# A hybrid decoder trunk on one core: the first Strassen step of each FFN takes two products of plain blocks first, and sums of weight blocks are made when first asked for

## The chip, the core and the metric

The kernel runs on one core of a Trainium2 chip. A time is that of one execution of the whole program on the device, in microseconds (us). The core's engines run side by side and wait for each other through semaphores: PE (matrix products), DVE and ACT (elementwise work), POOL (a little elementwise work) and SP (it issues nearly all DMAs). Each engine takes its instructions strictly in the order in which the program lists them.

## The reference

One step of a decoder trunk of two layers over 544 tokens (512 of a prompt, 32 of eight sampled sequences). Each layer has two half-weighted SwiGLU FFNs around a mixer, four FFNs in all, and ends in a gated embedding:

```python
def swiglu(x, w1, w3, w2):
    return (jax.nn.silu(x @ w1) * (x @ w3)) @ w2
...
h = h + 0.5 * swiglu(rmsnorm(h, ffn1_norm[i]), ffn1_w1[i], ffn1_w3[i], ffn1_w2[i])
```

The model width is 1024 and the FFN width 2816. The mixer of layer 0 is a chunked gMLP, that of layer 1 an attention with forget gates whose K and V come once from the end of layer 0.

## The kernel before, in words

**Values in two parts.** All of it is float32. An operand is split into a rounded part `hi` (a cast on ACT, L190 for weights) and the rest `lo` (a subtraction on DVE, L191), and a product is three passes: hi·hi, hi·lo, lo·hi. So each 128x1024 piece of weights costs a DMA, one cast and one subtraction before PE can use it.

**An FFN.** It starts with four plain products over all of K (`tile_mm`: L233, L237, L239, 48 matmuls each), which make the first 256 of the 2816 hidden columns. The other 2560 come in ten steps of 256 columns (`ffn_steps`, L476), each by the Strassen-Winograd scheme: seven products of 24 matmuls instead of eight. Each step handles W1 and W3 together. Products are named by the digits "1" to "7":

- "1", "2", "4" multiply plain weight blocks a11, a12, a22. "5" takes a21+a22, "6" takes ("5" - a11), "7" takes a11-a21, "3" takes a12 - "6" (`seven`). Each such sum is one DVE instruction of 1.22 us (L176, in `_sum`).
- They add up in three accumulators of PSUM: "1", "6", "7", "4" in A, "5", "3" in C (both of the pool `ps`, three buffers, which the four plain products use too), "2" in B (two buffers of the pool `pb`).
- What "1", "6" and "5" leave in A and C is copied out by ACT (L484, here r1, r6, r5) before the next product adds to the same accumulator. So "6" waits for r1 and "7" for r6.

**The order of weights.** `ffn_pieces` lists all pieces in the order in which PE takes them; `prepare` runs ahead in that list. Before unit u it splits pieces up to u+2, makes sums up to u+3, and issues the loads that piece u+6 needs:

```python
p = self.pieces[min(u + load, end)]
need = [x for x in (p["sum"][::2] if p["sum"] else [p["src"]]) if isinstance(x[1], int)]
```

A raw block that was not asked for in this way is loaded when its split or sum asks for it (`_raw`). Raw blocks are loaded in the order a11, a21, a22, a12.

**The order of work.** The four plain products are ordered by a scheduler, and the steps behind them stand as the code issues them. On DVE and ACT the start of an FFN is full: besides casts, subtractions and sums there are the input forms of the seven products (`forms`, L299 on ACT, L303 to L306 and L278 on DVE, L277 on ACT; four times) and the gates of the plain columns (L418 to L421), and L418 and L420 are what frees the `ps` buffers of the plain products. In the first FFN SP reads a page table into registers between DMAs (48 register loads, L914).

Of the kernel before, what the change touches and what calls it, by code (L numbers as in the profile page):

```python
# [26 lines left out]
ALU = mybir.AluOpType  # L27
# [25 lines left out]
NKP = NC_ // 2  # L53

SEVEN = "1562734"


ORDER = """
# [28 lines left out]
class Builder:  # L87
# [37 lines left out]
    def set_stream(self):  # L125
        self.chain, self.pending, self.bg, self.pages = None, [], [], {}
        self.aps, self.raws = [], {}
        self.pieces, self.sums, self.split = [], {}, {}
        self.p_next = self.p_split = self.p_sum = self.a_load = 0
        self.ahead = (2, 2, 4)  # L130
        self.pins = 0
# [9 lines left out]
    def seven(self, aps):  # L141

        r = len(self.aps)
        self.aps.extend(aps[k] for k in (0, 2, 3, 1))
        a11, a21, a22, a12 = ((r + k, 0) for k in range(4))
        d = {k: dict(key=(r, k), src=x, sum=None) for k, x in (("1", a11), ("2", a12), ("4", a22))}
        for k, x, op, y in (("5", a21, "+", a22), ("6", (r, "5"), "-", a11), ("7", a11, "-", a21),
                            ("3", a12, "-", (r, "6"))):
            d[k] = dict(key=(r, k), sum=(x, op, y))
        for v in d.values():  # L150
            v.update(n=1024)
        return d

    def _load(self):
# [12 lines left out]
    def _sum(self):  # L167
        p = self.pieces[self.p_sum]
        self.p_sum += 1
        if p["sum"] is None:  # L170
            return
        a, op, b = p["sum"]
        get = lambda x: self._raw(x, 1024) if isinstance(x[1], int) else self.sums[x]
        a, b = get(a), get(b)
        t = self.flat(1024)
        self.nc.vector.tensor_tensor(t, a, b, ALU.add if op == "+" else ALU.subtract)  # L176
        self.sums[p["key"]] = t

    def _split(self):
        while self.p_sum <= self.p_split:  # L180
# [181 lines left out]
    def ffn_slots(self):  # L362


        out, tail = [], len(PARTS) - 1
        for j in range(1, NPAIR):
            ws = [("w", p, c, None) for p, c in BETWEEN.get(j, ())]
            gs = [("g", j, k, None) for k in SEVEN]
            early = j % 2 == 1
            for n, g in enumerate(gs):  # L370
                out.append(g)
                if ws and n in ((0, 2, 4, 6) if early else (3, 4, 5, 6)):
                    out.append(ws.pop(0))
            assert not ws
        n = 2 * PARTS[tail]
        out += [("w", tail, c, range(n - 2)) for c in range(3)] + [("w", tail, c, range(n - 2, n)) for c in range(3)]
        return out + [("w", tail, c, None) for c in range(3, NC_)]
# [1007 lines left out]
```

## Time and profile before

| | |
|---|---|
| median of 3 runs | 2092.44 us (2092.16 to 2092.45) |
| the profiled execution | 2092.14 us, its span 2090.4 us (1.7 us lie outside the span) |
| mean granted TensorE clock | 0.997 of full speed |
| busy PE, DVE, ACT | 98%, 73%, 45% of the span |

The span runs from the first to the last instruction in the trace, and all positions below are us from its start. A row of the order of time names an engine's instruction and, in brackets, how long the engine had been idle before it and which instruction ended that.

### The profile page before, as it was taken

How to read it: one execution, taken by the hardware profiler on the slowest of the kernel's cores; microseconds unless marked ns; L12 is line 12 of the kernel's file. 1: busy time of each engine (PE TensorE's matmuls, PEld its weight loads, DVE VectorE, ACT ScalarE, POOL GpSimd, SP SyncE). 2: the span in 40 equal slices, each digit the busy share in tenths (PEclk: the TensorE clock that was granted, in tenths of full speed). 3: DMA queues.
4: the chain of work that ended last, by engine and by line, in shares of the span. 5: the costliest groups of instructions: out<-in, count | busy, mean ns of one | idle time of the engine just before them, and what ended most of it. 6: DMA issues, size and time to landing. Idle time of an engine off the chain costs nothing.

```text
span 2090.4 us, 38801 instructions
## 1 busy us (share of the span) xinstructions
PE 2056.4 (98%) x16364; PEld 2019.2 (97%) x16364; DVE 1521.3 (73%) x1893; ACT 935.0 (45%) x1376; POOL 179.0 (9%) x226
## 2 busy tenths in 40 slices
PE   7999999999999999999999999999999999999999
PEld 6999999999999999999999999999977999999999
DVE  7877787556787777776698777786465787777873
ACT  6444344423445344454355344444364654343451
POOL 0000000410100000042050000001041300000020
PEclk9999999999999999999999999999999999999999
DMA  4232324312223232432194332326467322322331
GB/s 162 91 112 71 111 92 141 104 54 71 72 101 117 73 105 81 152 97 81 48 327 143 111 101 91 112 78 198 158 197 264 102 102 71 111 83 99 123 102 44
DMA packets 93776, 237.94 MB, mean 114 GB/s; under 512 B 9490, under 2 KB 27442, under 8 KB 93602
## 3 DMA queue, kind: packets, MB, share of 16 engines
q1 hardware_dynamic: 93458, 235.42, 33.8%
q8 instruction: 129, 2.11, 0.4%
q14 instruction: 45, 0.37, 0.1%
q10 hardware_dynamic: 144, 0.04, 0.0%
HBM read 218.94 MB, written 16.49 MB: 113 GB/s over the span
## 4 chain that ended last, share of the span: by engine, by line
PE 89%; DVE 5%; ACT 3%; issue 1%; DMA 1%; POOL 1%; SPq 0%; ACTq 0%; DVEq 0%; POOLq 0%
PE ps L476 33%; PE ps L233 14%; PE ps L239 14%; PE ps L237 14%; PE pb L476 5%; ACT big L190 1%; DVE big L191 1%; DVE big L176 1%; PE ps L1144 1%; PE ps L1146 1%; PE ps L1145 1%; PE ps L992 0%; PE ps L990 0%; PE ps L1105 0%; ACT big L277 0%
## 5 line engine op out<-in xcount | busy, mean ns | idle before, releaser
L476 PE MATMUL ps<-big,big 128*128 128x272 f32 x5760 | 749.6, 289 | 9.7 <-ACT tmp L484 6.2
L476 PEld LDWEIGHTS ps<-big,big 128*128 128x128 f32 x5760 | 735.2, 189 | 11.5 <-ACT tmp L484 7.7
L191 DVE TENSOR_TENSOR big<-big,big 128x1024 fp32r<-128x1024 f32 (+2 forms) x541 | 594.1, 1100 | 101.2 <-ACT big L190 100.5
L190 ACT CAST big<-big 128x1024 fp32r<-128x1024 f32 (+2 forms) x541 | 489.2, 931 | 280.5 <-DVE big L176 275.7
L233 PE MATMUL ps<-big,big 128*128 128x256 f32 x2768 | 577.2, 290 | 13.9 <-ACT big L190 7.2
L237 PE MATMUL ps<-big,big 128*128 128x256 f32 x2768 | 571.8, 287 | 0.0
L239 PE MATMUL ps<-big,big 128*128 128x256 f32 x2768 | 571.6, 288 | 0.0
L233 PEld LDWEIGHTS ps<-big,big 128*128 128x128 f32 x2768 | 444.4, 189 | 17.3 <-ACT big L190 7.2
L237 PEld LDWEIGHTS ps<-big,big 128*128 128x128 f32 x2768 | 446.9, 189 | 0.0
L239 PEld LDWEIGHTS ps<-big,big 128*128 128x128 f32 x2768 | 443.5, 188 | 0.9 <-issue 0.4
L318 POOL TENSOR_TENSOR st<-st,tmp 128x544 f32<-128x544 f32 (+1 forms) x63 | 86.5, 1373 | 1611.6 <-ACT tmp L316 1611.3
L176 DVE TENSOR_TENSOR big<-big,big 128x1024 f32<-128x1024 f32 x160 | 194.9, 1218 | 0.0
L515 DVE SCALAR_TENSOR_TENSOR big<-ps,big 128x544 f32<-128x544 f32 x160 | 115.5, 722 | 106.8 <-PE ps L239 106.7
L484 ACT COPY tmp<-ps 128x544 f32<-128x544 f32 x120 | 73.5, 613 | 146.5 <-PE ps L476 146.2
L476 PE MATMUL pb<-big,big 128*128 128x272 f32 x960 | 127.1, 288 | 0.0
L448 ACT ACTIVATE big<-big 128x544 f32<-128x544 f32 x80 | 52.8, 661 | 161.8 <-DVE big L445 160.7
L476 PEld LDWEIGHTS pb<-big,big 128*128 128x128 f32 x960 | 123.2, 188 | 0.0
L289 ACT ACTIVATE big<-big,gains 128x544 fp32r<-128x544 f32 (+1 forms) x80 | 56.0, 704 | 124.3 <-DVE big L515 64.9
L445 DVE TENSOR_TENSOR big<-big,st 128x1088 f32<-128x1088 f32 x80 | 103.2, 1290 | 10.0 <-ACT big L498 8.5
L278 DVE TENSOR_TENSOR big<-big,big 128x544 fp32r<-128x544 f32 (+1 forms) x96 | 69.5, 724 | 28.8 <-ACT big L277 28.3
L290 DVE SCALAR_TENSOR_TENSOR big<-big,gains,big 128x544 fp32r<-128x544 f32 (+1 forms) x80 | 64.0, 804 | 27.7 <-ACT big L289 27.7
L277 ACT CAST big<-big 128x544 fp32r<-128x544 f32 (+1 forms) x96 | 61.9, 644 | 26.4 <-DVE big L769 14.9
(189 smaller groups left out, 1269.6 us busy)
## 6 DMA issues: line engine op xcount, KB each, us to landing
big<-in_w SPq DMA_DIRECT2D x160, 512.0 KB
big<-in_w2a SPq DMA_DIRECT2D x64, 512.0 KB
big<-in_w2b SPq DMA_DIRECT2D x32, 384.0 KB
big<-in_w13p SPq DMA_DIRECT2D x16, 512.0 KB
big<-in_win SPq DMA_DIRECT2D x16, 512.0 KB
big<-in_wg SPq DMA_DIRECT2D x16, 512.0 KB
big<-in_wkv SPq DMA_DIRECT2D x16, 512.0 KB
big<-in_ck SPq DMA_DIRECT2D x16, 512.0 KB
```

The lines of the kernel that those rows point to most:

```text
L176: self.nc.vector.tensor_tensor(t, a, b, ALU.add if op == "+" else ALU.subtract)
L190: self.nc.scalar.copy(hi, src)
L191: self.nc.vector.tensor_tensor(lo, src, hi.bitcast(F32), ALU.subtract)
L233: i = nc.tensor.matmul(out[:, a:b], wh, xh[:, a:b], start=s, stop=False)
L237: nc.tensor.matmul(out[:, a:b], wh, xl[:, a:b], start=False, stop=False)
L239: nc.tensor.matmul(out[:, a:b], wl, xh[:, a:b], start=False, stop=e)
L278: self.nc.vector.tensor_tensor(pair[:, 1, cols], src, pair[:, 0, cols].bitcast(F32), ALU.subtract)
L318: nc.gpsimd.tensor_tensor(acc[:, cols], acc[:, cols], sq, ALU.add)
L445: tt(g, g, rstd.unsqueeze(1).broadcast_to([P, 2, T]), ALU.mult)
L476: nc.tensor.matmul(dst[w], a[:, c], b, start=k in "152" and kp == 0 and n == 0, stop=kp == NKP - 1 and n == 2, skip_group_check=True)
L484: nc.scalar.copy(t["r" + k], t["C" if k == "5" else "A"])
L515: nc.vector.scalar_tensor_tensor(h[c], whole(out), 0.5, h[c], ALU.mult, ALU.add)
```

## The change

The ten steps of an FFN took the products in the order 1 5 6 2 7 3 4. The first step of each FFN now takes them as 1 2 6 5 7 3 4; the other nine stay. A sum that is needed before its own place in the list is made on the spot, with the sums it rests on, since "6" now stands ahead of "5". The count of instructions of every engine stays the same, and so do the bytes loaded.

```diff
--- before.py
+++ after.py
@@ -54,6 +54,8 @@
 
 SEVEN = "1562734"
 
+FIRST = "1265734"
+
 
 ORDER = """
 q0 K3 K2 K0 q1 q2 q3 K1 s0123 n2 n3 n1 q4 f1 p1 q5 q6 f0 n0 q7 p2 p0 f3 f2 a0 s4567 p3 t0 a1 v0 a2
@@ -125,7 +127,7 @@
     def set_stream(self):
         self.chain, self.pending, self.bg, self.pages = None, [], [], {}
         self.aps, self.raws = [], {}
-        self.pieces, self.sums, self.split = [], {}, {}
+        self.pieces, self.sums, self.defs, self.split = [], {}, {}, {}
         self.p_next = self.p_split = self.p_sum = self.a_load = 0
         self.ahead = (2, 2, 4)
         self.pins = 0
@@ -149,6 +151,7 @@
             d[k] = dict(key=(r, k), sum=(x, op, y))
         for v in d.values():
             v.update(n=1024)
+            self.defs[v["key"]] = v
         return d
 
     def _load(self):
@@ -167,14 +170,20 @@
     def _sum(self):
         p = self.pieces[self.p_sum]
         self.p_sum += 1
-        if p["sum"] is None:
-            return
-        a, op, b = p["sum"]
-        get = lambda x: self._raw(x, 1024) if isinstance(x[1], int) else self.sums[x]
-        a, b = get(a), get(b)
-        t = self.flat(1024)
-        self.nc.vector.tensor_tensor(t, a, b, ALU.add if op == "+" else ALU.subtract)
-        self.sums[p["key"]] = t
+        if p["sum"] is not None:
+            self._form(p)
+
+    def _form(self, p):
+
+        key = p["key"]
+        if key not in self.sums:
+            a, op, b = p["sum"]
+            get = lambda x: self._raw(x, 1024) if isinstance(x[1], int) else self._form(self.defs[x])
+            a, b = get(a), get(b)
+            t = self.flat(1024)
+            self.nc.vector.tensor_tensor(t, a, b, ALU.add if op == "+" else ALU.subtract)
+            self.sums[key] = t
+        return self.sums[key]
 
     def _split(self):
         while self.p_sum <= self.p_split:
@@ -365,7 +374,7 @@
         out, tail = [], len(PARTS) - 1
         for j in range(1, NPAIR):
             ws = [("w", p, c, None) for p, c in BETWEEN.get(j, ())]
-            gs = [("g", j, k, None) for k in SEVEN]
+            gs = [("g", j, k, None) for k in (FIRST if j == 1 else SEVEN)]
             early = j % 2 == 1
             for n, g in enumerate(gs):
                 out.append(g)
```

Where instructions stand now, at three places in the first FFN. The names carry the program's buffer numbers, which differ a little between the two programs, and the lines of the change are 9 higher.

**SP**, the loads of the first Strassen step's raw blocks; 175 is a11 (issued earlier), 258 is a21, 260 is a22, and a12 is 262 before and 409 in the change. Before:

```order
L157 DMA big_258<-in_w 128x1024
L157 DMA big_260<-in_w 128x1024
L157 DMA big_262<-in_w 128x1024
L914 TENSOR_LOAD pt
L914 ISA x2
...
L1241 DMA big_348<-in_passed 128x512
```

In the change:

```order
L160 DMA big_258<-in_w 128x1024
L160 DMA big_260<-in_w 128x1024
L923 TENSOR_LOAD pt
L923 ISA x2
...
L1250 DMA big_344<-in_passed 128x512
...
L160 DMA big_409<-in_w 128x1024
```

TENSOR_LOAD with its ISA row is one register load from the page table. Before, the three blocks are issued together, and 14 register loads follow up to in_passed. In the change a12 stands behind 15 register loads, in_passed and 5 more. The plain products are units 0 to 3 and "1" is piece 4. Before, unit 1 asks for piece 7, "2", and so for a12; in the change piece 7 is "5", which needs a21 and a22 alone, and a12 is asked for at unit 3, by the split of "2", now piece 5.

**DVE**, from the subtraction of "1" (the first row) to the forms of the last kp (the last row). Before, 414 is the subtraction of "5"; in the change 412 is that of "2". Before:

```order
L191 TENSOR_TENSOR big_341<-big_175,big_340 128x1024
L176 TENSOR_TENSOR big_344<-big_258,big_260 128x1024
L303 TENSOR_TENSOR tmp_402<-big_399 128x544
L305 TENSOR_TENSOR tmp_403<-big_399,tmp_402 128x272
L306 TENSOR_TENSOR tmp_403<-big_399,tmp_403 128x272
L278 TENSOR_TENSOR big_404<-tmp_402,big_404 128x544
L278 TENSOR_TENSOR big_405<-tmp_403,big_405 128x544
L191 TENSOR_TENSOR big_414<-big_344,big_413 128x1024
L176 TENSOR_TENSOR big_417<-big_344,big_175 128x1024
L303 TENSOR_TENSOR tmp_473<-big_470 128x544
```

In the change:

```order
L200 TENSOR_TENSOR big_339<-big_175,big_338 128x1024
L312 TENSOR_TENSOR tmp_398<-big_395 128x544
L314 TENSOR_TENSOR tmp_399<-big_395,tmp_398 128x272
L315 TENSOR_TENSOR tmp_399<-big_395,tmp_399 128x272
L287 TENSOR_TENSOR big_400<-tmp_398,big_400 128x544
L287 TENSOR_TENSOR big_401<-tmp_399,big_401 128x544
L200 TENSOR_TENSOR big_412<-big_409,big_411 128x1024
L184 TENSOR_TENSOR big_415<-big_258,big_260 128x1024
L184 TENSOR_TENSOR big_417<-big_415,big_175 128x1024
L312 TENSOR_TENSOR tmp_473<-big_470 128x544
```

The sum of "5" (344 before, 415 in the change) moved from ahead of the third forms to behind the subtraction of the step's second product, where it stands together with the sum of "6" (417 in both).

**ACT**, the casts and copies of the step, from the last cast of the gates on. Before, the casts are those of "6", "2", "7", "3" and "4" (520, 524, 559, 595, 627), and the copies are r1, r5 and r6 in this order:

```order
L277 CAST big_490<-tmp_485 128x544
L190 CAST big_520<-big_417 128x1024
L190 CAST big_524<-big_262 128x1024
L484 COPY tmp_557<-ps_495 128x544
L190 CAST big_559<-big_528 128x1024
L484 COPY tmp_593<-ps_532 128x544
L190 CAST big_595<-big_563 128x1024
L484 COPY tmp_625<-ps_495 128x544
L190 CAST big_627<-big_260 128x1024
```

In the change the casts are those of "6", "5", "7", "3" and "4" (520, 524, 560, 598, 629), and the copies are r1, r6 and r5:

```order
L286 CAST big_490<-tmp_485 128x544
L199 CAST big_520<-big_417 128x1024
L199 CAST big_524<-big_415 128x1024
L493 COPY tmp_558<-ps_495 128x544
L199 CAST big_560<-big_528 128x1024
L199 CAST big_598<-big_564 128x1024
L493 COPY tmp_627<-ps_495 128x544
L199 CAST big_629<-big_260 128x1024
L493 COPY tmp_659<-ps_602 128x544
```

The cast of "2" is gone from here, since it is earlier now, and that of "5" came. The copy r5 moved behind r6; r6 stands behind one cast more than r1 or two ("7", and now "3").

## Rows read from the trace of the kernel before

**Rows 1.** The page: busy time of each engine with its share of the span and its count of instructions, and the shares of the chain that ended last by engine.

```profile
PE 2056.4 (98%) x16364; PEld 2019.2 (97%) x16364; DVE 1521.3 (73%) x1893; ACT 935.0 (45%) x1376; POOL 179.0 (9%) x226
...
PE 89%; DVE 5%; ACT 3%; issue 1%; DMA 1%; POOL 1%; SPq 0%; ACTq 0%; DVEq 0%; POOLq 0%
```

**Rows 2.** The waits of PE over the whole span: engine and line, what it waited for, total us, times, longest.

```profile
PE ps L476 <- ACT tmp L484: 6.2, 7, 2.0
PE ps L233 <- DVE tmp L418: 4.2, 1, 4.2
PE ps L476 <- DVE tmp L418: 3.5, 1, 3.5
```

**Rows 3.** PE in order of time at the first Strassen step of the first FFN: start, us, engine, line, operation, out<-in, forms, how many, and in brackets the idle time before it and what ended that. These are the products "1", "5", "6", "2", and from 59.62 on "7" and what follows without a pause.

```profile
40.22 3.18 PE L476 MATMUL ps<-big,big 128*128 128x272 f32 x24
46.87 4.52 PE L476 MATMUL ps<-big,big 128*128 128x272 f32 x24 [3.47 <-DVE tmp L418]
52.11 3.28 PE L476 MATMUL ps<-big,big 128*128 128x272 f32 x24 [0.72 <-ACT tmp L484]
55.22 3.19 PE L476 MATMUL pb<-big,big 128*128 128x272 f32 x24
59.62 12.57 PE L476 MATMUL ps<-big,big 128*128 128x272 f32 x98 [1.20 <-ACT tmp L484]
```

**Rows 4.** DVE in order of time in the same stretch, columns as in rows 3.

```profile
36.92 1.23 DVE L191 TENSOR_TENSOR big<-big,big 128x1024 fp32r<-128x1024 f32 x1 [0.23 <-ACT big L190]
38.06 1.22 DVE L176 TENSOR_TENSOR big<-big,big 128x1024 f32<-128x1024 f32 x1
...
42.61 1.23 DVE L191 TENSOR_TENSOR big<-big,big 128x1024 fp32r<-128x1024 f32 x1
43.76 1.22 DVE L176 TENSOR_TENSOR big<-big,big 128x1024 f32<-128x1024 f32 x1
44.89 0.72 DVE L303 TENSOR_TENSOR tmp<-big 128x544 f32<-128x544 f32 x1
...
46.00 0.72 DVE L418 TENSOR_TENSOR tmp<-ps,st 128x544 f32<-128x544 f32 x1
...
50.64 2.36 DVE L191 TENSOR_TENSOR big<-big,big 128x1024 fp32r<-128x1024 f32 x2 [0.23 <-ACT big L190]
...
55.25 1.23 DVE L191 TENSOR_TENSOR big<-big,big 128x1024 fp32r<-128x1024 f32 x1 [1.11 <-ACT big L190]
56.39 1.22 DVE L176 TENSOR_TENSOR big<-big,big 128x1024 f32<-128x1024 f32 x1
```

**Rows 5.** ACT in order of time in the same stretch.

```profile
41.53 1.05 ACT L190 CAST big<-big 128x1024 fp32r<-128x1024 f32 x1
42.48 1.39 ACT L299 ACTIVATE big<-big,gains 128x544 f32<-128x544 f32 x2
...
49.56 1.99 ACT L190 CAST big<-big 128x1024 fp32r<-128x1024 f32 x2
51.45 0.60 ACT L484 COPY tmp<-ps 128x544 f32<-128x544 f32 x1
...
58.01 1.05 ACT L190 CAST big<-big 128x1024 fp32r<-128x1024 f32 x1 [2.28 <-DVE big L176]
58.96 0.60 ACT L484 COPY tmp<-ps 128x544 f32<-128x544 f32 x1
```

**Rows 6.** The DMAs that SP issues in the first 60 us, merged by line and tile; the second number is the time from the first issue to the end of the last one of the row, and SP's register loads are not shown by this view.

```profile
13.93 5.81 SPq L157 DMA_DIRECT2D big<-in_w13p  x2
19.78 9.35 SPq L157 DMA_DIRECT2D big<-in_w  x4
37.05 0.33 SPq L1241 DMA_DIRECT2D big<-in_passed  x1
```

**Rows 7.** POOL in order of time: the first reader of the tile that the DMA in_passed fills.

```profile
40.83 0.51 POOL L1244 CAST neg<-big 128x384 fp32r<-128x384 f32 x1 [27.47 <-DMA big<-in_passed]
```

**Rows 8.** Stretches of the span: from:to, length, busy time of PE, weight loads, DVE, ACT and POOL with their counts, granted TensorE clock (1.00 is 2.4 GHz, 0.50 is 1.2 GHz), share of the DMA engines, GB/s. The first two follow the issue at 13.93.

```profile
15.00:17.20 2.20, 2.20 (x19) 2.20 (x19) 1.99 (x4) 2.20 (x6) 0.00 (x0) 1.00 0.64 225
17.20:19.40 2.20, 2.20 (x20) 2.20 (x19) 1.89 (x4) 2.20 (x5) 0.00 (x0) 1.00 0.00 0
```

**Rows 9.** Stretches of the span, columns as in rows 8, behind three pauses of PE.

```profile
32.64:36.05 3.41, 3.41 (x15) 3.41 (x16) 2.88 (x6) 3.14 (x5) 0.00 (x0) 0.50 0.17 70
...
46.87:49.71 2.84, 2.84 (x12) 2.84 (x13) 2.75 (x6) 1.96 (x4) 0.00 (x0) 0.50 0.97 392
...
1688.10:1691.50 3.40, 3.40 (x17) 3.40 (x17) 2.29 (x3) 1.56 (x2) 0.00 (x0) 0.50 0.00 0
```

**Rows 10.** PE in order of time at the first Strassen step of the second FFN (products "1" and "5" in one row, "6", "7" and on) and, last, product "6" of the fourth FFN.

```profile
574.83 6.19 PE L476 MATMUL ps<-big,big 128*128 128x272 f32 x48
581.18 3.28 PE L476 MATMUL ps<-big,big 128*128 128x272 f32 x24 [0.16 <-ACT tmp L484]
...
588.33 3.90 PE L476 MATMUL ps<-big,big 128*128 128x272 f32 x29 [0.84 <-ACT tmp L484]
...
1687.20 4.80 PE L476 MATMUL ps<-big,big 128*128 128x272 f32 x24 [1.98 <-ACT tmp L484]
```

**Rows 11.** DVE in order of time in the second FFN, where the difference of a split waits for its cast.

```profile
571.69 1.23 DVE L191 TENSOR_TENSOR big<-big,big 128x1024 fp32r<-128x1024 f32 x1 [1.12 <-ACT big L190]
```

## The prediction

> **What bounds the kernel now.** I read the page first. PE is busy for 98% of the span and carries 89% of the chain that ended last [rows 1]; 2090.4 - 2056.4 leaves 34 us for all its pauses. Work that stays the same can therefore be made shorter only by taking pauses away, or the half clock behind them. The waits of PE come next [rows 2]: 6.2 us in seven waits of Strassen products for a copy out of PSUM (L484), 3.5 us in one wait of a Strassen product for L418, which frees a `ps` buffer, and 4.2 us in a wait of a plain product for L418 that lies ahead of the change's place. The second is the one that the new order touches most directly: "5" stands second now and must have a `ps` buffer, while "2" needs one of `pb`.
>
> The order of time shows where it lies [rows 3]: "5" starts at 46.87 after 3.47 us of pause and takes 4.52 us, where "1" took 3.18. Then "6" waits 0.72 for r1 and "7" 1.20 for r6, and behind 59.62 no pause follows. So everything that this stage does to the end is read at one point: when "7" starts.
>
> What sets "6" is the next question, since it stands third in both orders. DVE has hardly a gap from 36.92 to 50.64 [rows 4]; ACT has the cast of "6" at 49.56 and right behind it the copy r1, 51.45 + 0.60 = 52.05 [rows 5], and "6" starts at 52.11. The start of "6" thus goes by the chain of sums, forms, gates and casts on DVE and ACT, and not by how early PE is done with the product ahead of it.
>
> **Part 1: the load of a12 in the first FFN.** Before, a12 is the last of four loads whose issue ends at 29.13; a single issue takes 0.33, so it stands at 28.8 [rows 6]. The order of SP in the change puts 20 register loads and in_passed ahead of it. Fourteen register loads took 37.05 - 29.13 = 7.92 us [rows 6], so 0.566 each. The new issue stands at 28.8 + 20 x 0.566 + 0.33 = 40.45, 11.7 us later. Nothing waits in these register loads that a faster engine could shorten.
>
> From issue to use I have two prices. in_passed, of half the size, was issued at 37.05 and its first reader, POOL, started at 40.83 [rows 7]: 3.78. The two loads issued from 13.93 on moved their bytes by 17.2, behind which the DMA engines stand still [rows 8]: about 3.2. I take 3.5, since the queue is as empty at 40.45 as in these two cases, and keep 3.2 and 3.8 as ends. So a12 is there at 43.95. The Trainium skill (DMA: Bandwidth & Descriptors, Rules for kernel authors) advises to issue a DMA early, compute, and wait late; this edit does the reverse. By that rule the load is exposed, as the rows have it; were the load hidden all the same, the sum would be that of the second rival below.
>
> The cast of "2" stands on ACT where that of "5" stood, at 41.53 [rows 5], and now waits for 43.95. ACT and DVE work in order, so the forms and gates behind it wait too. The subtraction came 1.08 us behind its cast (41.53 to 42.61), and what follows it comes at a pace of 1.15 [rows 4]. So: subtraction 45.03; sum of "5" 46.18; sum of "6" 47.33, plus 0.2 because it now needs the result of the instruction right ahead of it (between nothing and 0.31, the overlap of 0.08 between neighbours plus the 0.23 that DVE waits at 36.92 for a result of ACT [rows 4]); the forms at 47.53 + 1.15 = 48.68, where they were at 44.89. That is 3.8 us, and the chain behind moves along: "6" starts at 52.11 + 3.8 = 55.9.
>
> PE in the meantime: "1" as before to 43.4, "2" from about 45.0, and even at half clock (24 x 0.227 = 5.45, from 15 matmuls in 3.41 us [rows 9]) it is done by 50.5. Then PE stands for more than 5 us, and "6" begins at half clock. What this costs, three places show: "5" 4.52 - 3.08 = 1.4 (98 matmuls take 12.57 us, so 24 take 3.08 [rows 3]); 15 x (0.227 - 0.128) = 1.5 behind the pause of 4.2 [rows 2, 9]; 4.80 - 3.2 = 1.6 in the fourth FFN [rows 10], with a granted clock of 0.50 in each [rows 9]. I take 1.6, as this pause is the longest; the upper end is a whole product at half clock, 5.45 - 3.08 = 2.4. Below, r6 sets the end: from the cast of "6" (49.56) to the end of r6 (59.56) lie 10.0 us [rows 5], so "7" can't start before 49.56 + 3.8 + 10.0 = 63.4.
>
> "6" and "5" then take 6.16 + 1.6 from 55.9, and "7" starts at 63.6 where it stood at 59.62: **+4.0 us** for the first FFN, between +3.25 and +5.2 with the ends above. The pause at "5" (3.47) and its half clock don't come back, as they lie ahead of the start of "6".
>
> **Part 2: the second FFN.** In the other three FFNs no register loads stand on SP, and a12 comes in time. In the second, "6" waits 0.16 and "7" 0.84 [rows 10]. DVE waits 1.12 us there for a cast at 571.69 [rows 11], between the subtraction of "5" and its sum; with "2" second, this subtraction still waits, but the sums and forms behind move up against the casts. I take the 0.16 and half of the 0.84: **-0.6 us**, between -1.0 and nothing.
>
> **Part 3: the third and fourth FFN.** The same counts of casts, sums and forms stand ahead of "6"; only the two sums of "5" and "6" now stand behind each other, 0.2 us each as above: **+0.4 us** in the two, between nothing and 0.6.
>
> **Part 4, at nothing.** The edit of `_sum` makes no other instruction. The copy r5, now behind r6, has all of "7" (3.1 us) to be done before "3" needs its accumulator; without that cover it would cost its 0.60. The cast of "3" ahead of r6 is inside the 10.0 us above.
>
> **Sum:** 4.0 - 0.6 + 0.4 = +3.8 on the profiled 2092.14 us, thus 2095.9. The three runs have a median 0.3 above the profiled execution, so 2096.2 in their terms. The ends: 3.25 - 1.0 = +2.3 and 5.2 + 0.6 = +5.8, so 2094.7 and 2098.2. About 0.2%, 4.2 us, is what a measurement of this kernel can tell from no change, and the forecast lies just inside it.
>
> **The rivals.** *The half clock lasts longer, and it is slower by over 0.2%.* Place: PE at "6" and "5" of the first FFN, behind more than 5 us of pause and a "2" that ran at half clock itself. For it speaks that no row of before has two such pauses so close; against it that all three pauses cost 1.4 to 1.6. It decides from a cost of 2.0 us on, with the other terms as taken (+4.2); with all of "6" at half clock it is 2.4, and +4.6 or 2097.0, up to 2098.2 with the other ends. A load that takes 3.8 brings it on from 1.7 already.
>
> *The load is in time, and nothing is left to measure.* If SP gets through its register loads faster or the cast of "2" stands later than 40.6, "6" starts at 52.11 + 0.2, and "7" near the 59.6 that r6 allows: -0.2 to +0.4 in sum, about 2092.4. Against it: the 0.566 comes from fourteen of these same loads in the same place.
>
> *Faster.* If the pause of "5" for `ps` is the loss itself, taking "2" first gives back 3.47 and 1.4: 2092.44 - 4.9 = 2087.6. The Trainium skill has a sentence for this (Perfetto Trace Analysis, Optimization Strategy): consistent bubbles on the engine that should be saturated "can mean there isn't enough SBUF/PSUM for the next tile to be allocated". The trace agrees as to the one wait of 3.5 us [rows 2]. Against it: r1 ends at 52.05 whatever PE does ahead of it, and the pause only moves to "6". It decides if "6" starts before 48.
>
> **How the numbers follow.** The forecast up to +4.2 has 0.56, slower by the half clock or a longer load 0.35, in time 0.06, faster 0.03. The likeliest case's own range is 2094.7 to 2096.6. The range goes from 0.3 below its lower end (the distance of profile and runs) to the top of the slower rival, 2094.4 to 2098.2; the two cases below it leave out 0.09, and some 0.05 lies above. The time is 2096.2. By 0.2%: faster 0.03, same 0.62, slower 0.35.
>
> **What the profile after would show.** SP's row for a12 alone near 40.4, behind in_passed; the cast of "2" on ACT near 44 with an idle time that the load ended; the forms behind the two sums near 48.7; in PE's order "1" at 40.22, "2" near 45, a pause of about 5 us that r1 ends, "6" near 55.9 and above 4.5 us long, "7" near 63.6; the second FFN's "6" without a wait. The load is refuted as the cause if ACT casts "2" near 41.5; the chain on DVE and ACT if "6" starts at 52 though the load was late; and the sum is wrong if more than 1 us moves in an FFN other than the first.

## The result, and the profile after

The changed kernel took 2095.48 us (median of 22 runs), the kernel before 2092.28 in 22 runs beside it. That is 3.2 us more by the medians; the ratio is 1.0017 with a 95% interval of 1.0011 to 1.0023, which is some 3.6 us (2.3 to 4.8). The time lies inside the forecast's range (2094.4 to 2098.2); the ratio is under the 0.2% that the forecast named, though the interval reaches above it. The profiled execution took 2094.79 us against 2092.14, +2.65, and has a span of 2093.0. Busy times stayed (PE 2056.6 us where it was 2056.4 [rows 1]), so the loss stands in PE's pauses: span less busy time is 36.4 us where it was 34.0.

Of the waits of PE over the span (as in [rows 2]) the largest of a Strassen product:

```profile
PE ps L485 <- ACT tmp L493: 11.1, 5, 6.7
```

The wait of a Strassen product for L418 (now L427), 3.5 us, is gone; those for the copies (L493) grew from 6.2 to 11.1 us, and 6.7 of them is one wait. Where it lies, PE in order of time at the first step of the first FFN shows, to be laid beside [rows 3]; the rows are "1", "2" in two pieces, and from 54.98 on "6", "5" and part of what follows:

```profile
41.11 3.18 PE L485 MATMUL ps<-big,big 128*128 128x272 f32 x24
44.25 0.77 PE L485 MATMUL pb<-big,big 128*128 128x272 f32 x4
45.51 2.79 PE L485 MATMUL pb<-big,big 128*128 128x272 f32 x20 [0.49 <-DVE big L200]
54.98 13.20 PE L485 MATMUL ps<-big,big 128*128 128x272 f32 x90 [6.68 <-ACT tmp L493]
```

"1" starts 0.9 us later than before, behind plain products that stood longer at half clock in this execution (to 38.1 where it was 35.9). PE then waits 6.68 us ahead of "6" all the same, so this delay doesn't reach "6". "6" starts at 54.98 where it stood at 52.11. Of the single matmuls in the last row, the 25th ("5") starts at 59.72 and the 49th ("7") at 62.74, where "7" stood at 59.62: +3.1 us. SP's DMAs, ACT and DVE (beside [rows 4 to 6]) say why:

```profile
19.23 8.77 SPq L160 DMA_DIRECT2D big<-in_w  x3
36.48 0.33 SPq L1250 DMA_DIRECT2D big<-in_passed  x1
39.67 16.55 SPq L160 DMA_DIRECT2D big<-in_w  x5
```

```profile
43.14 1.05 ACT L199 CAST big<-big 128x1024 fp32r<-128x1024 f32 x1 [2.43 <-DMA big<-in_w]
...
52.43 1.99 ACT L199 CAST big<-big 128x1024 fp32r<-128x1024 f32 x2
54.32 0.60 ACT L493 COPY tmp<-ps 128x544 f32<-128x544 f32 x1
...
61.46 0.61 ACT L493 COPY tmp<-ps 128x544 f32<-128x544 f32 x1
```

```profile
44.23 1.23 DVE L200 TENSOR_TENSOR big<-big,big 128x1024 fp32r<-128x1024 f32 x1 [2.75 <-ACT big L199]
45.37 2.48 DVE L184 TENSOR_TENSOR big<-big,big 128x1024 f32<-128x1024 f32 x2
47.77 0.72 DVE L312 TENSOR_TENSOR tmp<-big 128x544 f32<-128x544 f32 x1
```

The load of a12 is the first of the five at 39.67. ACT's cast of "2" waits 2.43 for it, DVE waits 2.75 for that cast, then makes both sums, and the forms stand at 47.77 where they were at 44.89. "6" begins when r1 is done, 54.32 + 0.60. The clock of the first 3.4 us of "6", and of the 3.4 behind:

```profile
54.98:58.38 3.40, 3.40 (x15) 3.40 (x16) 2.29 (x3) 1.05 (x1) 0.00 (x0) 0.50 0.37 116
58.38:61.78 3.40, 3.40 (x28) 3.40 (x28) 2.98 (x5) 1.27 (x2) 0.00 (x0) 0.96 0.36 114
```

In the second FFN ("1", then "6" with "5", then "7" and on, beside [rows 10]) the wait of "6" is gone and that of "7" is shorter. The last row is the start of "6" in the fourth FFN:

```profile
577.85 3.17 PE L485 MATMUL ps<-big,big 128*128 128x272 f32 x24
...
583.88 6.22 PE L485 MATMUL ps<-big,big 128*128 128x272 f32 x48
590.67 5.54 PE L485 MATMUL ps<-big,big 128*128 128x272 f32 x42 [0.58 <-ACT tmp L493]
...
1689.84 3.47 PE L485 MATMUL ps<-big,big 128*128 128x272 f32 x15 [2.37 <-ACT tmp L493]
```

By PE's positions the account of the two profiled executions is: +3.1 at "7" of the first FFN, +3.0 at "1" of the second (577.85 - 574.83), +2.3 at its "7" (590.67 - 588.33), and +2.6 at "6" of the fourth (1689.84 - 1687.20).

### The profile page after: what moved, and what is told of

Its sections match the earlier page's. It is cut to its first block, busy times and chain, and to the rows that moved or that the text cites. A ratio compares the mean times of both kernels' runs of the same rounds, so it can differ in the third digit from the quotient of the medians.

```text
span 2093.0 us, 38766 instructions
## 1 busy us (share of the span) xinstructions
PE 2056.6 (98%) x16364; PEld 2019.7 (97%) x16364; DVE 1522.6 (73%) x1893; ACT 934.6 (45%) x1376; POOL 178.8 (9%) x226
## 4 chain that ended last, share of the span: by engine, by line
PE 90%; DVE 4%; ACT 2%; DMA 1%; issue 1%; SPq 1%; POOL 1%; ACTq 0%; DVEq 0%; POOLq 0%
PE ps L485 34%; PE ps L242 15%; PE ps L248 15%; PE ps L246 14%; PE pb L485 5%; ACT big L199 1%; SPq L923 1%; PE ps L1153 1%; PE ps L1155 1%; PE ps L1154 1%; DVE big L200 1%; PE ps L1001 0%; PE ps L999 0%; DVE big L184 0%; PE ps L1114 0%
## 5 line engine op out<-in xcount | busy, mean ns | idle before, releaser
L485 PE MATMUL ps<-big,big 128*128 128x272 f32 x5760 | 749.2, 289 | 11.1 <-ACT tmp L493 11.1
L493 ACT COPY tmp<-ps 128x544 f32<-128x544 f32 x120 | 73.5, 613 | 148.5 <-PE ps L485 148.5
```

Source lines behind the costliest of these rows:

```text
L485: nc.tensor.matmul(dst[w], a[:, c], b, start=k in "152" and kp == 0 and n == 0, stop=kp == NKP - 1 and n == 2, skip_group_check=True)
L493: nc.scalar.copy(t["r" + k], t["C" if k == "5" else "A"])
```

## The experiments

All were compared with the kernel before on the same chip. The times of the kernel before beside them were 2092.26, 2091.98 and 2091.74 in three groups; intervals of a ratio are about 0.001 to either side (0.0014 in the two kernels with five runs), so a difference under 2 us is read from the traces and not from times. Two single runs, 10442.29 us of the kernel before in the first group and 3698.65 us of the run with the copies moved, stand far outside and leave the medians as they are.

**The load of a12 early.** In the changed kernel, the first FFN asks for a12 together with a21 and a22:

```diff
+        if p["key"] == (4, "5"):
+            need.append((7, 0))
```

> The changed kernel with the load of a12 in the first FFN issued directly behind those of a21 and a22, ahead of the register loads, as before; every other order is that of the change. Theory (the late load is the cause): the cast of "2" stands near 40.5 to 41.5 instead of 43.1, the forms near 45, "6" near 52.2 instead of 55.0; PE then pauses some 6 us ahead of "6" and pays 1.6 for half clock, so "7" starts near 60 and the time is 2092.0 to 2092.8, level with before. Rival (the new order of sums and casts itself delays "6"): "6" stays near 55 and the time at 2095.5.

It took 2091.85 us, ratio 1.0001 (0.9991 to 1.0010): as far as times can tell, the loss is gone with the load's lateness, in the new order of products. Every engine but SP has its instructions in the order of the change. In order of time, ACT at the cast of "2", and PE at "1" and from "6" on:

```profile
40.73 1.04 ACT L199 CAST big<-big 128x1024 fp32r<-128x1024 f32 x1
```

```profile
41.29 3.17 PE L487 MATMUL ps<-big,big 128*128 128x272 f32 x24
...
52.55 15.68 PE L487 MATMUL ps<-big,big 128*128 128x272 f32 x101 [5.07 <-ACT tmp L495]
```

"6" is back at 52.55, 0.44 behind its old place. PE still pauses 5.07 us there, so the new order hardly moves its start; it moves the pause from "5" to "6". In this execution the half clock behind the pause cost 2.7 us ("7" at 61.42, less 52.55 and 6.16), and "7" was later than before by 1.8. That this execution was level with before all the same has another reason: "1" of the second FFN was 1.7 late, "1" of the third 1.0, and "1" of the fourth 0.6 early. The 1.6 us between the last two are a stretch of the attention near 1632 that ran at half clock in the kernel before (and in the change) and at full clock here. The kernel before and then this one, columns as in rows 8:

```profile
1630.00:1634.00 4.00, 4.00 (x22) 4.00 (x21) 1.73 (x2) 1.21 (x2) 3.84 (x8) 0.57 0.01 4
```

```profile
1630.00:1634.00 4.00, 3.86 (x31) 3.86 (x32) 2.39 (x3) 2.17 (x3) 4.00 (x9) 1.00 0.14 56
```

No instruction was moved there. So the trace shows "6" back and the load's part gone, 2.43 us; it doesn't show the new order as free in the first FFN, where this execution lost 1.7 us and the half clock cost 2.7. The times, level to some 2 us, leave room for that.

**The load of a12 late in the old order.** In the kernel before, unit 1 of the first FFN asks for a22 alone, so that a12 comes where the split or a later unit asks for it:

```diff
+        if p["key"] == (4, "2"):
+            need = [(6, 0)]
```

> The kernel before, in its old order of products, with the load of a12 alone issued late in the first FFN, behind the register loads as in the change or a little later. Theory (the late load costs only because "2" now stands second and its cast heads ACT's line): a12 is first asked for by the cast near 50.6, so nothing moves: "6" at 52.1, "7" at 59.6, 2092.3. Rival (a late load costs by itself, by pushing the next loads or by sharing the DMA engines with them): 1 us or more, 2093.3 to 2095.5.

It took 2091.67 us, ratio 1.0000 (0.9991 to 1.0009). "6", "2" and "7" stand where they stood, though a12 is now the first of the five loads that SP issues from 40.87 on. SP's DMAs, and PE at "6" and from "7" on:

```profile
40.87 9.38 SPq L157 DMA_DIRECT2D big<-in_w  x5
```

```profile
52.13 3.29 PE L478 MATMUL ps<-big,big 128*128 128x272 f32 x24 [1.98 <-ACT tmp L486]
...
59.63 8.56 PE L478 MATMUL ps<-big,big 128*128 128x272 f32 x66 [1.18 <-ACT tmp L486]
```

So by the times, to some 2 us, neither part costs by itself: the order with an early load is level, the late load with the old order is level, and both together cost 3 us.

**The load later still.** In the changed kernel a12 is loaded twice into one tile:

```diff
+        if self.a_load == 7:
+            self.nc.sync.dma_start(out=raw[:, :ap.shape[1]], in_=ap)
         self.raws[self.a_load] = raw
```

> The changed kernel with a12 of the first FFN loaded twice into the same tile, the second load issued when the first has landed, so that the data is there some 3.3 us later than in the change. Theory (the chain load, cast of "2", sums, forms, cast of "6", r1 sets the start of "6" one to one): "6" moves from 55.0 to 58.3 and the time by +3.3 to 2098.8. Rival (the load is not what the chain waits for, or slack absorbs it): under +1, 2095.5 to 2096.5.

It took 2099.24 us, ratio 1.0039 (1.0024 to 1.0053), 3.8 over the change. SP's second issue, the cast of "2" and PE from "6" on:

```profile
43.60 0.33 SPq L162 DMA_DIRECT2D big<-in_w  x1
```

```profile
47.13 1.04 ACT L201 CAST big<-big 128x1024 fp32r<-128x1024 f32 x1 [5.73 <-DMA big<-in_w]
```

```profile
58.95 9.21 PE L487 MATMUL ps<-big,big 128*128 128x272 f32 x57 [5.25 <-ACT tmp L495]
```

The cast came 3.99 later than in the change and "6" 3.97 later. From the start of the cast of "2" to the start of "6" lie 11.84 us in the change, 11.82 with the early load and 11.82 here: a chain without slack, passed on one to one. Of the 3.99, 0.44 come from the first issue, which stood at 40.11 in this execution (39.67 in the change), and 3.49 lie between the two issues, where 3.3 were expected; SP was through with the register loads between them at 42.7 and issued nothing until 43.60.

**The clock at "6".** Products of no use keep PE at work ahead of "6" in the first FFN of the changed kernel; N is 22 in the first run and 37 in the second:

```diff
+            if k == "6" and j == 1 and not self.warmed:
+                self.warmed = True
+                t["C"] = self.ps()[:, :, :HT]
+                for n in range(N):
+                    nc.tensor.matmul(t["C"][:, n % 2], self.onesr, xf[0]["1"][0], start=True, stop=True,
+                                     skip_group_check=True)
```

> The changed kernel with 22 extra matrix products of no use put on PE ahead of "6" in the first FFN, into the accumulator that "5" clears afterwards; they start when the gates have freed that accumulator (near 50.2) and should end near 54.7. Theory (half clock behind the long pause costs 1.6 us): the granted clock at "6" is full, "6" takes 3.1 instead of 4.7, and the time falls by up to 1.6 to 2093.9; it can't fall further, since r6 bounds "7". Rival (r6, and not PE's speed, sets "7"): "6" is quicker but "7" starts where it did, 2095.5.

> As e_warm, but with 37 extra matrix products of no use ahead of "6" in the first FFN: in e_warm the 22 ran at full clock, ended 2.3 us ahead of "6", and "6" began at half clock all the same. Now they should run from about 48.6 to 53.4, up to the start of "6". Theory (half clock behind the pause costs 1.6): the granted clock of "6" and "5" is full, their 48 products take 6.2 instead of 7.8, and the time is 1.0 to 1.6 under the change, 2093.9 to 2094.5; less where r6 then bounds "7" (it stood 0.7 ahead of "7"). Rival (the clock at "6" does not go by what PE did before it): 2095.5.

The first took 2093.63 us, 1.9 under the change, but not for the reason given. Its products ended 2.28 us ahead of "6", and "6" was at half clock all the same (0.57 in the window 54.98 to 58.38, 18 matmuls). The profiled execution (2093.78, 1.0 under that of the change) was quicker because its cast of "2" stood at 42.07, 1.07 earlier than in the profile of the change, with "6" at 53.91: again 11.84 behind. What made up the rest of the 1.9 isn't shown. ACT at that cast, and PE at the products of no use and from "6" on:

```profile
42.07 1.05 ACT L200 CAST big<-big 128x1024 fp32r<-128x1024 f32 x1 [1.22 <-DMA big<-in_w]
```

```profile
48.58 3.05 PE L485 MATMUL ps<-big,onesr 128*128 128x272 f32 x22 [1.35 <-DVE tmp L428]
53.91 14.33 PE L492 MATMUL ps<-big,big 128*128 128x272 f32 x100 [2.28 <-ACT tmp L500]
```

The second took 2093.49 us. Here the products fill the pause up to 0.38 us. PE at the products of no use, at "6" with "5", and from "7" on, and the stretch from the start of "6":

```profile
48.49 4.95 PE L485 MATMUL ps<-big,onesr 128*128 128x272 f32 x37 [1.36 <-DVE tmp L428]
53.83 6.32 PE L492 MATMUL ps<-big,big 128*128 128x272 f32 x48 [0.38 <-ACT tmp L500]
60.97 11.22 PE L492 MATMUL ps<-big,big 128*128 128x272 f32 x88 [0.82 <-ACT tmp L500]
```

```profile
53.80:57.20 3.40, 3.37 (x26) 3.38 (x27) 2.28 (x3) 1.05 (x1) 0.00 (x0) 1.00 0.38 108
```

"6" and "5" take 6.32 us at full clock, where "6" alone took 4.74 in the change. From the same start of "6" (53.91 and 53.83), "7" stands at 61.55 without and at 60.97 with the full clock: only 0.6 of the 1.5 us is kept, since r6 now bounds "7" (a wait of 0.82), as the prediction's floor had it. The two times, 2093.63 and 2093.49, can't be told apart. In both the extra products also moved a few instructions of the attention, far behind.

**The other three FFNs alone.** The new order in all FFNs but the first:

```diff
-            gs = [("g", j, k, None) for k in (FIRST if j == 1 else SEVEN)]
+            gs = [("g", j, k, None) for k in (FIRST if j == 1 and n > 0 else SEVEN)]
```

> The new order of products in the second, third and fourth FFN only; the first keeps the old order and its load. Theory (all of the loss is the first FFN's load; the rest is -0.6 in the second FFN and +0.2 in each of the other two): 2092.0 to 2092.3, not to be told from before, with "6" of the second FFN without a wait and "7" waiting 0.58. Rival (the new order of casts and sums costs in every FFN): 2093 or more.

It took 2091.70 us, ratio 0.9997 (0.9988 to 1.0006), and its second FFN reads as in the change ("6" without a wait, "7" with 0.58):

```profile
581.02 6.22 PE L486 MATMUL ps<-big,big 128*128 128x272 f32 x48
587.82 8.43 PE L486 MATMUL ps<-big,big 128*128 128x272 f32 x65 [0.58 <-ACT tmp L494]
```

**The copies earlier.** With the load early, can the new order gain? r1 and r6 are put behind their products:

```diff
-            after.append(lambda: evict(j, k))
+            if j == 1 and k in "16":
+                evict(j, k)
+            else:
+                after.append(lambda: evict(j, k))
```

> The order of the change with the early load of a12, and in the first step of each FFN the copies r1 and r6 stand on ACT right behind their product in the program, so ahead of the casts of "6" and "5" (r1) and of "3" (r6). Theory (with "2" second PE is through "1" and "2" long before "6", and "6" waits only for where r1 stands on ACT): "6" starts when the cast of "6" is done, near 51.2 instead of 52.5 in the first FFN, and the waits for r1 and r6 in the other three FFNs (0.6, 0.6, 0.8 and 2.4 in the change) fall to half; 2089.0 to 2090.5. Rival (the casts and subtractions themselves bound "6"): under 0.7 is gained, 2091.3 to 2092.3.

It took 2091.59 us, ratio 1.0000 (0.9991 to 1.0010): no gain in time. "6" did move, to 50.47, and now waits for its cast. ACT at r1 and at the casts of "6" and "5", PE from "6" on, and the stretches behind its start:

```profile
46.02 0.61 ACT L498 COPY tmp<-ps 128x544 f32<-128x544 f32 x1
...
49.38 1.99 ACT L199 CAST big<-big 128x1024 fp32r<-128x1024 f32 x2
```

```profile
50.47 21.74 PE L487 MATMUL ps<-big,big 128*128 128x272 f32 x149 [4.69 <-ACT big L199]
```

```profile
50.47:53.90 3.43, 3.43 (x13) 3.12 (x14) 3.43 (x3) 0.90 (x1) 0.00 (x0) 0.50 0.10 8
53.90:57.30 3.40, 3.40 (x20) 3.40 (x19) 2.28 (x3) 1.63 (x2) 0.00 (x0) 0.62 0.42 151
```

But "6" and most of "5" ran at half clock, 2.8 us in sum ("7" at 59.47, less 50.47 and 6.16), so "7" was only 0.15 earlier than before. In the second and third FFN new waits for the cast and the subtraction of "6" took the place of those for the copies. In the fourth the wait ahead of "6" fell from 2.37 to 0.92 us and the clock behind it was full (1.00 from 1686 to 1700, where the change has 0.84 from 1689 to 1700): from its "1" to the end of the span lie 410.2 us, where the change has 411.7.

The same copies in the old order of products, with the old load:

> The old order of products and the old load, with the copies r1 and r6 of the first step of each FFN right behind their products. Theory (it is the pause behind "2" that the new order makes long, and its half clock, that hold e_copies back): in the old order the pause ahead of "6" is short and nothing is at half clock behind it beyond "5", so "6" moves up from 52.1 to the end of "5" near 51.4 and "7" by 0.7 to 1.5; 2091.0 to 2091.7. Rival (the new order is what makes room for the copies): 2092.3, no change.

It took 2092.12 us, ratio 1.0001 (0.9992 to 1.0010). The copies move "7" up by 1.9 us here too (57.68), so the new order isn't what makes room for them; 1.1 of it is lost at the next product but one ("4"), which waits for DVE, and what is left, 0.7 us at "1" of the second FFN (574.11), is too small for a time. PE at "7" with "3", and at "4":

```profile
57.68 6.19 PE L476 MATMUL ps<-big,big 128*128 128x272 f32 x48
64.94 1.25 PE L476 MATMUL ps<-big,big 128*128 128x272 f32 x8 [1.07 <-DVE big L496]
```

**Copies, load and clock together.** As with the copies above in the new order, with 24 products of no use ahead of "6":

> Order of the change, early load of a12, the copies r1 and r6 right behind their products (as in e_copies), and 24 products of no use on PE ahead of "6" in the first FFN. In e_copies "6" began at 50.47, 1.6 us before its place in the old kernel, but the clock was half for "6" and most of "5", some 2.7 us, and "7" stood only 0.3 earlier. Theory (the half clock ate what the order and the copies gained): "6" at 50.5 at full clock, "7" near 56.9 to 57.5 where it stood at 59.6; 2089.3 to 2090.3, 1.3 to 2.3 under e_copies and faster than either kernel. Rival (DVE and ACT bound "7" anyway): "7" waits for its cast or subtraction (done near 56.3) or for r6; 2091 to 2092.

It took 2090.29 us, ratio 0.9992 (0.9983 to 1.0001): 1.3 under the copies alone, but the interval still holds 1. "6" begins at 50.24 at full clock and "7" at 57.14, 2.5 earlier than before; "4" then waits 0.44 for DVE. PE in order of time from "6" on:

```profile
50.24 0.77 PE L494 MATMUL ps<-big,big 128*128 128x272 f32 x4 [0.32 <-ACT big L200]
51.50 11.83 PE L494 MATMUL ps<-big,big 128*128 128x272 f32 x92 [0.49 <-DVE big L201]
63.77 2.40 PE L494 MATMUL ps<-big,big 128*128 128x272 f32 x17 [0.44 <-DVE big L514]
```

**Less work ahead of "6".** The gate of the second pair of plain columns is called in the step loop, behind "2", and not before the steps:

```diff
+            if n == 1:
+                plain()
+                hid[0, 1] = first[1]
```

> As e_copies, and the gate of the second pair of plain columns in each FFN (two products of L427 and L429, the silu, the product, one cast, one subtraction) stands behind the product "2" of the first step instead of ahead of the last input forms. Only the new order of products allows it: the gate frees the accumulator of "5", which now comes after "6". Theory (DVE and ACT work ahead of "6" sets its start): 2.9 us of DVE leave the chain ahead of "6" in the first FFN, "6" starts near 48.5, and the pause of 5 us and the half clock behind it are mostly gone; the work comes back behind "6", where DVE has pauses; with smaller gains in the other FFNs 2086 to 2089. Rival (the work only moves, and "7" or "3" waits by as much as "6" gains): the time of e_copies.

> As e_gate, but with the copies r1 and r6 where the change has them. If the copies' places count only together with the gate's, or the other way round, this run and e_copies show it: by the first theory alone (copies) it is no faster than 2091.9; by the second alone (gate) it is within 1 us of e_gate; where the two add, it lies 1.5 to 3 above e_gate.

Both expectations missed. With the copies moved it took 2095.07 us, ratio 1.0011 (1.0002 to 1.0020), 3.5 over the copies alone. "6" did start at 48.94, 1.5 earlier than with the copies alone, but what left the chain ahead of it came back behind it: "3" waits at 61.17 for the copy r5 and "4" at 65.15 for DVE, and 0.2 us are left when the second step begins (68.24 and 68.42). The loss lies behind this stage. In the second FFN the waits grew to 0.32, 0.95 and 0.70, and "1" of the third is 1.5 later than with the copies alone; "1" of the fourth, with the third FFN and the attention between, is 3.9 later. PE in order of time:

```profile
48.94 0.76 PE L488 MATMUL ps<-big,big 128*128 128x272 f32 x4 [2.35 <-ACT big L199]
...
61.17 3.29 PE L488 MATMUL ps<-big,big 128*128 128x272 f32 x24 [0.66 <-ACT tmp L499]
65.15 7.13 PE L488 MATMUL ps<-big,big 128*128 128x272 f32 x55 [0.69 <-DVE big L508]
```

With the copies unmoved it took 2103.58 us, ratio 1.0054 (1.0041 to 1.0068): the silu of the moved gate now stands ahead of r1 on ACT, waits 3.31 us there for DVE, and r1 comes at 54.39 behind it. Its profiled execution took 2108.0, and beside the profile of the early load "1" of the second FFN is 2.5 later, that of the third 4.3 and that of the fourth 12.7. ACT in order of time:

```profile
52.39 0.66 ACT L430 ACTIVATE tmp<-tmp 128x544 f32<-128x544 f32 x1 [3.31 <-DVE tmp L429]
...
54.39 0.61 ACT L496 COPY tmp<-ps 128x544 f32<-128x544 f32 x1
```

What the program lists ahead of r1 there was left out of that expectation. With the copies moved, the edit also put some instructions of the attention in another order; with the copies unmoved it did not. In both most of the loss lies behind the first FFN, so the two times are not of this stage alone, and why the later stages lost isn't shown.

## Why the prediction came out right

**The load of a12** was the cause, with the size and by the way described. Issue 39.67 (40.45 was predicted), cast 43.14 (43.95), forms 47.77 (48.7), "6" 54.98 (55.9), "7" 62.74 (63.6): the first FFN lost 3.1 us where 4.0 were forecast. Nearly all of the 0.9 is in the first figure: SP was done with a22 at 28.00 in this execution, where the working took 28.8 from the one profile of before. From issue to cast it took 3.47 us (3.5 predicted; 3.42, 3.53 and 3.53 in three experiments), and the two sums took 2.40 from start to forms, 0.1 less than assumed. The advice of the Trainium skill to issue early and wait late (DMA: Bandwidth & Descriptors, Rules for kernel authors) agrees with the four kernels (before, the change, the early load, the late load in the old order): the late issue cost 3 us where the wait came early, and nothing that a time shows where it came late.

**The chain on DVE and ACT** as what sets "6": shown by the 11.82 to 11.84 us between the cast of "2" and "6" in four kernels whose casts lie 6.4 us apart, and by "6" at 52.55 with the early load though PE was done with "2" 5.07 us ahead of it. The 2.87 us by which "6" came later have two parts: the cast of "2" stood 1.61 later than that of "5" had (43.14 and 41.53), and the way from this cast to "6" is 1.26 longer than before (11.84 and 52.11 - 41.53 = 10.58), since the sum of "5" now stands in it, as the working had it. With the early load the cast stood 0.80 earlier than that of "5" had, and 0.44 was left. That the pause of 3.47 us at "5" would not come back was right: it is now part of the 6.68 at "6".

**The half clock** cost 1.6 in the profiled execution, as taken (62.74 - 54.98 - 6.16). As a size it is less settled than the working had it: behind pauses of 2.3 to 6.7 us in the changed order it cost 1.5, 1.6, 1.8, 2.7 and 2.8 in five kernels, and the ceiling of one product (2.4) didn't hold, since "5" was slowed as well. Nor is the whole 1.6 a part of the loss: r6 would have held "7" back without it, and the full clock gave back 0.6. The way from the cast of "6" to the end of r6 was 9.6 us (52.43 to 62.07), where the working took 10.0. The time of the rival "slower by over 0.2%", from 2096.5 on, was reached by five of the 19 runs that lie together and by the three apart from them (below), though no trace of one of these shows its cause; the median stayed under it.

**The second FFN** gained 0.7 from "1" to "7" (0.6 predicted), the third lost 0.2 (its two waits grew from 0.35 and 0.94 to 0.63 and 0.83), and up to the fourth 0.1 more was lost: together +0.3 against +0.4. These three can't be told from nothing by a time, as the run with the new order in them alone shows.

**Luck in the number.** By PE's positions the terms add up to +2.7 us (3.1 - 0.7 + 0.3) where +3.8 was forecast, 1.1 less. That the median lies only 0.7 under the 2096.2 is in part luck: the profiled execution of the change is 0.7 under its own median, that of the kernel before 0.1 under its own. What the runs lose beyond the traced 2.7 isn't shown.

**The rival "faster"** is refuted by the early load: with nothing late, the new order takes 2091.85 and not 2087.6, and "6" starts at 52.55 and not before 48. The 3.5 us that a Strassen product waited for a buffer of PSUM were a pause that another wait took over; the sentence of the Trainium skill on consistent bubbles (Perfetto Trace Analysis, Optimization Strategy) names a want of buffers as a possible cause of a gap that repeats; this wait came once, and taking it away gained nothing. **The rival "load in time"** gives the right time for the kernel with the early load (2092.4 and 2091.85) and nearly the right start of "6" (52.3 and 52.55); but it had "7" near 59.6, and "7" stood at 61.42, so its time came out in part by the 1.6 us that the attention gained.

What was wrong lies in the experiments: that less work ahead of "6" would help. What was moved behind "6" was waited for there: of the 1.5 us gained at "6", 0.2 was left at the second step.

## What to carry to other kernels

Before two steps are swapped, follow each operand of the step that comes first back to the place where its load is issued, and count what stands ahead of it on the issuing queue; here the swap alone and the late load alone were each level with before to some 2 us, and together they cost 3 us. An engine that works in order passes the wait of one cast on to everything behind it, one to one, until a chain with slack is met; the distance between two such instructions, the same to 0.02 us in several kernels, shows such a chain better than a time does.

## What was not expected of the hardware

The changed kernel's runs seem to spread more: 19 of the 22 lie between 2093.57 and 2097.58 and three between 2100.61 and 2101.90, while 18 of the 22 beside them of the kernel before lie between 2090.77 and 2092.76. The later groups don't bear this out: of 27 runs of the kernel before, 23 lie between 2090.02 and 2093.52 in the first and 25 between 2089.99 and 2093.32 in the second, nearly as wide. Two things in the traces vary from execution to execution and act on the new order alone or more strongly: the place at which SP issues behind its register loads (the last of the three loads of a11, a21 and a22 was out at 26.8 to 28.5 in five profiles), and the cost of the half clock behind the long pause (1.5 to 2.8). The half clock varies outside the change's reach too, as the attention near 1632 shows. That these two make a spread is argued from single profiles, not shown run by run.
